# Attention scores of a head pair as two 64-row contractions in the two halves of the TensorE array

## The chip, the cores and the metric

The kernel runs on one core of one Trainium2 chip. The metric is device time in microseconds (us) of one execution, as the median of several runs. All times inside an execution come from one profiled execution, counted from the start of its span.

## What is computed

One layer of a hybrid model over 512 latent tokens (a grid of 8 rows by 64 columns) with 256 context tokens: a normalised input is projected, and two branches run in parallel, a state-space recurrence with a gated unit, and neighbourhood attention with 8 heads of 64 channels. The branches are merged and projected, and an expert retrieval (PEER) follows. The change lies in the attention. Cut from the reference to that:

```python
def na_mixer(q, k, v, k_ctx, v_ctx, rpb):
    ...
        s_lat = jnp.einsum('bhqd,bhkd->bhqk', q_row, k_band).astype(jnp.float32) * scale + bias
        s_ctx = jnp.einsum('bhqd,bhkd->bhqk', q_row, k_ctx).astype(jnp.float32) * scale
        prob = jax.nn.softmax(jnp.concatenate([s_lat, s_ctx], axis=-1), axis=-1).astype(v.dtype)
        return (jnp.einsum('bhqk,bhkd->bhqd', prob[..., :n_band], v_band)
                + jnp.einsum('bhqk,bhkd->bhqd', prob[..., n_band:], v_ctx))
```

The contraction over `d` has 64 terms for each head.

## The kernel before

**Where attention stands.** The whole layer is one program. A scheduler orders the instructions of every engine ahead of time from a timeline of its own; on the chip each engine then takes its instructions in that fixed order and waits where a semaphore is not set. The projections of keys, values and queries (`project`, L453) run on TensorE (PE) while VectorE (DVE) walks a recurrence of 95 dependent steps (`scan_step`, L588 to L595, four small operations on the tile `E` for each step). After its last step the states are copied from `E` to `S` (L618 on POOL, L619 on ScalarE, ACT), and the pool of `E` is closed. The space then holds `Y`, `gt` and `k0`, the tiles of `y_load` and `y_part` (L636 to L661), the readout of the recurrence: eight parts, each with one load of `gt` and eight small loads of `k0` on the SP queue, two buffers of each, and 12 matmuls into the bank `yy` (L657).

**The attention loop.** The 32 items are 4 tiles of 128 queries by 8 heads, heads fastest. For an item i, `att_a(i)` (L677) computes scores: 128 queries by 256 neighbourhood keys (L685) and by 256 context keys (L686) into one of the three `mm` banks; DVE adds the bias tile `bs` (L687) and takes the negated row maximum `nm` (L689); ACT takes the exponential into `P` (L691). `att_b(i)` transposes `P` in four pieces on PE into a `tp` bank (L698), and ACT and DVE copy a half each to `PT` (L700, L701). `att_c` multiplies `PT` by the values for the two heads of a pair at once: 8 matmuls, alternating between the lower and the upper 64 output rows (L716), into bank `kk` or `mc`. After eight heads `att_norm` divides by the sums (L719 to L734). The loop issues `att_b(i)`, `att_a(i + 2)`, now and then a `y_part`, then `att_c(i)`.

**The query tiles.** A 128-row tile of `kT` holds the keys of two heads, 64 rows each. Each head has a query tile of its own, `qT[h]`, 128 rows of which 64 are zero (memset on POOL, L628; copy on ACT, L629). So a score matmul contracts 128 rows, half of them against zeros:

```python
        ql = qT[h][:, m * 128:(m + 1) * 128]
        pe.matmul(s_[:, 0:256], ql, kT[h // 2][:, m:m + 2].rearrange("p j x -> p (j x)"), start=True, stop=True)
        pe.matmul(s_[:, 256:512], ql, kC[h // 2], start=True, stop=True)
```

These are 4-byte (f32) operands, and the trace records one such matmul as two weight loads and two matmuls.

**What follows.** When all eight `y_part` are done, `Y` is transposed (L771, into `tp`), which ends the use of the space of `Y`; `cb2` and the tiles `wm2` of `mod2` (L787 to L792: SP load, POOL product, ACT sum, two buffers, 32 times) come into the same space. Beside that the gated unit, the two branches and the merge run: 128-row matmuls of 512 columns in one helper (L445 to L447), whose weights are split by ACT and DVE (L174, L175). The order puts some of these matmuls into the end of the attention, ahead of the transposes of `Y`.

Of the kernel before, what the change touches and what calls it, by code (L numbers as in the profile page):

```python
# [10 lines left out]
F32 = mybir.dt.float32  # L11
# [5 lines left out]
AF = mybir.ActivationFunctionType  # L17
ALU = mybir.AluOpType
AX = mybir.AxisListType
# [15 lines left out]
NH = 8  # L35
# [51 lines left out]
def tile_hybrid(ctx, tc, A, out, dbg=None):  # L87
    nc = tc.nc
    sy, act, dve, gp, pe = nc.sync, nc.scalar, nc.vector, nc.gpsimd, nc.tensor

    def open_pool(**kw):
        cm = tc.tile_pool(reuse_waits="tile", **kw)
        return cm, cm.__enter__()

    def close_pool(*cms):
        for cm in cms:
            cm.__exit__(None, None, None)
# [13 lines left out]
    def bank(tag="mm", bufs=None):  # L111
        bufs = bufs or nb[tag]
        return (psA if tag in ("kk", "yy") else ps).tile([128, 512], F32, tag=tag, name=tag, bufs=bufs)
# [25 lines left out]
    ftcm, ftp = open_pool(name="ftp", bufs=1)  # L139
# [230 lines left out]

    def outer(eng, o, P, yr, yi, g0, n, tag, neg, pool):
        tmp = [pool.tile([128, n, TC, HG], F32, tag=f"{tag}{i}", name=f"{tag}{i}") for i in range(2)]
        xr, xi = (P[:, j, g0:g0 + n].rearrange("p g (m o) -> p g m o", o=1).to_broadcast([128, n, TC, HG])
                  for j in range(2))
        yr, yi = (y[:, g0:g0 + n].rearrange("p g (o h) -> p g o h", o=1).to_broadcast([128, n, TC, HG])
                  for y in (yr, yi))
        ov = [o[:, :, j].rearrange("p g (m h) -> p g m h", h=HG) for j in range(2)]
        cmul(eng, ov[0], ov[1], xr, xi, yr, yi, tmp, conj=neg)
# [197 lines left out]
    for o in SEQ1:  # L576
        m = nxt[o]
        nxt[o] += 1
        if o == "u":
            a, c = (a1, c1) if m == 1 else project(m, True)  # L580
# [21 lines left out]
    kT = [t[:, 0:640].rearrange("p (j x) -> p j x", x=128) for t in kTC]  # L602
    kC = [t[:, 640:] for t in kTC]
    Vt = [ftp.tile([128, 4, 512], F32, tag="ft", name=f"V{i}", bufs=4) for i in range(2)]
    V = [Vt[i // 4][:, i % 4] for i in range(7)]
    for m in range(4):
        a, c = project(8 + m, True)
# [3 lines left out]
        for j0, n in ((0, 4), (4, 3)):  # L611
            p = bank("tp")
# [5 lines left out]
        gp.tensor_copy(S[0:64, r], E[0:64, r, :, CC:CC + CL])  # L618
        act.copy(S[64:128, r], E[64:128, r, :, CC + CL - 1:CC - 1:-1])  # L619

    qt = [ftp.tile([128, 4, 512], F32, tag="ft", name=f"q{i}", bufs=4) for i in range(2)]
    qT = [qt[i // 4][:, i % 4] for i in range(NH)]
    for m in range(4):
        a, _ = project(12 + m, False)
        av = a.rearrange("p (r j c) -> p r j c", r=8, c=16)
        for e in range(2):
            s, z = slice(64 * e, 64 * e + 64), slice(64 * (1 - e), 64 * (1 - e) + 64)
            gp.memset(qT[2 * m + e][z], 0.0)  # L628
            act.activation(qT[2 * m + e][s].rearrange("p (j r c) -> p r j c", r=8, c=16), av[s], AF.Copy, scale=0.125)  # L629
    close_pool(ecm)  # L630

    ycm, yp = open_pool(name="yp", bufs=1, side="right")
# [32 lines left out]
    acm, ap_ = open_pool(name="ap", bufs=1)  # L665
    items = [(m, h) for m in range(4) for h in range(NH)]
    Pt, PTt, Ob, ssums = {}, {}, {}, {}

    def att_bias(i):
        m, h = items[i]  # L670
        bs = ap_.tile([128, 256], F32, tag="bs", name="bs", bufs=4)
        act.dma_start(bs, A["bias"][h, {0: 0, 3: 2}.get(m, 1)])
        return bs

    bss = {i: att_bias(i) for i in range(2)}

    def att_a(i):  # L677
        m, h = items[i]
        if h == 0:
            ssums[m] = ap_.tile([128, NH], F32, tag="ssum", name="ssum", bufs=2)  # L680
        if i + 2 < len(items):
            bss[i + 2] = att_bias(i + 2)
        s_ = bank()
        ql = qT[h][:, m * 128:(m + 1) * 128]
        pe.matmul(s_[:, 0:256], ql, kT[h // 2][:, m:m + 2].rearrange("p j x -> p (j x)"), start=True, stop=True)  # L685
        pe.matmul(s_[:, 256:512], ql, kC[h // 2], start=True, stop=True)  # L686
        dve.tensor_add(s_[:, 0:256], s_[:, 0:256], bss.pop(i))  # L687
        nm = ap_.tile([128, 1], F32, tag="nm", name="nm", bufs=4)
        dve.tensor_reduce(nm, s_, axis=AX.X, op=ALU.max, negate=True)  # L689
        P = ap_.tile([128, 512], F32, tag="P", name="P", bufs=2)  # L690
        act.activation(P, s_, AF.Exp, bias=nm, accum_out=ssums[m][:, h:h + 1])  # L691
        Pt[i] = P

    def att_b(i):
        P = Pt.pop(i)
        pt = bank("tp")
        for j in range(4):
            pe.transpose(pt[:, j * 128:(j + 1) * 128], P[:, j * 128:(j + 1) * 128], ident)  # L698
        PT = ap_.tile([128, 512], F32, tag="PT", name="PT", bufs=PTB)
# [36 lines left out]
    y_load(0)  # L736
    y_load(1)
    att_a(0)
    att_a(1)
    for i in range(len(items)):  # L740
        att_b(i)
        if i + 2 < len(items):
            att_a(i + 2)
        if i % 3 == 2 and i // 3 < 8:
            y_part(i // 3)
        att_c(i)
        if i % NH == 1 and i > NH:
            att_norm(i // NH - 1)
# [17 lines left out]
    for i in range(4):  # L766
        p = bank("tp")
# [76 lines left out]
    for o in MERGE:  # L844
        m = cnt[o]
# [106 lines left out]
    for half in range(2):  # L952
        p = bank("tp")
# [256 lines left out]
    av = gup[0].tile([128, 128], F32, name="av")  # L1210
# [88 lines left out]
    prev = None  # L1299
# [80 lines left out]
```

## Time and profile before

| | |
|---|---|
| median of 3 runs | 1874.2 us (1873.22 to 1884.75) |
| the profiled execution, its own time | 1876.31 us |
| its span, first to last instruction | 1874.5 us |
| PE, DVE, ACT, POOL busy over the span | 92%, 80%, 43%, 35% |
| attention, first transposes of `P` to last | 245.9 to 325.6 us |
| last step of the recurrence | 284.9 us |
| first and last part of the readout on PE | 312.4 and 350.6 us |
| last transposes of `Y` | 355.7 us |

A stretch of the program is read by the view that gives each engine's busy time in it, then by the chain of work that ended last, then by the timeline of the engine that the chain names. Matmuls overlap in the records (the duration of one is longer than the step to the next), so the cost of a group on PE is read from the chain, where pieces stand end to start.

### The profile page before, as it was taken

How to read it: one execution, taken by the hardware profiler on the slowest of the kernel's cores; microseconds unless marked ns; L12 is line 12 of the kernel's file. 1: busy time of each engine (PE TensorE's matmuls, PEld its weight loads, DVE VectorE, ACT ScalarE, POOL GpSimd, SP SyncE). 2: the span in 40 equal slices, each digit the busy share in tenths (PEclk: the TensorE clock that was granted, in tenths of full speed). 3: DMA queues.
4: the chain of work that ended last, by engine and by line, in shares of the span. 5: the costliest groups of instructions: out<-in, count | busy, mean ns of one | idle time of the engine just before them, and what ended most of it. 6: DMA issues, size and time to landing. Idle time of an engine off the chain costs nothing.

```text
span 1874.5 us, 27846 instructions
## 1 busy us (share of the span) xinstructions
PE 1727.8 (92%) x9941; PEld 1505.1 (80%) x9941; DVE 1499.0 (80%) x3111; ACT 808.0 (43%) x1276; POOL 659.0 (35%) x500
## 2 busy tenths in 40 slices
PE   4989879989999989997479999999999999999997
PEld 1778657767779989986369899999999999998885
DVE  7899995587669998999879788788888888884445
ACT  5362245455555435666433333333333333333333
POOL 3553201166523730010233445444445544440002
PEclk8999989999999999998589999999999999999998
DMA  7342114576744435757599899999999999994432
GB/s 278 114 135 83 62 54 112 175 262 210 254 147 148 143 110 159 216 172 212 146 383 361 293 331 329 341 353 350 321 344 357 319 338 347 327 346 144 127 113 79
DMA packets 186331, 426.18 MB, mean 227 GB/s; under 512 B 25552, under 2 KB 91216, under 8 KB 186192
## 3 DMA queue, kind: packets, MB, share of 16 engines
q1 hardware_dynamic: 84816, 231.44, 36.5%
q0 software_dynamic: 36864, 134.23, 20.0%
q10 hardware_dynamic: 64512, 58.73, 9.7%
q8 instruction: 78, 1.28, 0.3%
q14 instruction: 61, 0.50, 0.1%
HBM read 388.72 MB, written 35.62 MB: 226 GB/s over the span
## 4 chain that ended last, share of the span: by engine, by line
PE 71%; DVE 18%; DMA 4%; issue 3%; ACT 2%; POOL 2%; ACTq 0%; SPq 0%; DVEq 0%; POOLq 0%
PE acc L1251 9%; PE acc L1252 9%; PE acc L1253 9%; PE yy L447 5%; PE yy L445 5%; PE yy L446 5%; PE kk L447 5%; PE kk L445 5%; PE kk L446 5%; PE mm L447 2%; PE mm L446 2%; PE mm L445 2%; DVE E L595 2%; DVE ta L592 1%; DVE ta L594 1%
## 5 line engine op out<-in xcount | busy, mean ns | idle before, releaser
L174 ACT CAST whi<-wraw 128x1024 fp32r<-128x1024 f32 (+1 forms) x212 | 213.6, 1008 | 165.5 <-issue 49.9
L175 DVE TENSOR_TENSOR wlo<-wraw,whi 128x1024 fp32r<-128x1024 f32 (+1 forms) x174 | 225.1, 1294 | 56.9 <-ACT whi L174 49.4
L1134 POOL DMA_INDIRECT gu<-in_pu_dram,idx x128 | 173.8, 1357 | 262.5 <-DVE gj L1141 217.4
L1134 POOL DMA_INDIRECT gu<-in_pv_dram,idx x128 | 167.0, 1305 | 161.1 <-DVE gacc L1152 135.4
L1233 DVE TENSOR_TENSOR wlo<-wraw,whi 128x1024 fp32r<-128x1024 f32 x128 | 157.5, 1231 | 41.4 <-ACT whi L1232 37.6
L1152 DVE SCALAR_TENSOR_TENSOR gacc<-gu,av,gacc 128x1024 f32<-128x1024 f32 x127 | 162.6, 1281 | 25.5 <-DMA gu<-in_pv_dram,idx 25.0
L447 PE MATMUL yy<-hth,wlo 128*128 128x384 f32 x512 | 174.9, 342 | 3.6 <-DVE wlo L175 3.6
L1141 DVE SCALAR_TENSOR_TENSOR gj<-gu,hrow 128x1024 bf16<-128x1024 f32 x128 | 156.0, 1219 | 23.4 <-DMA gu<-in_pu_dram,idx 22.9
L445 PE MATMUL kk<-hth,whi 128*128 128x384 f32 x512 | 173.3, 338 | 1.0 <-ACT ring L932 1.0
L445 PE MATMUL yy<-hth,whi 128*128 128x384 f32 x512 | 173.9, 340 | 0.0
L446 PE MATMUL yy<-htl,whi 128*128 128x384 f32 x512 | 173.9, 340 | 0.0
L447 PE MATMUL kk<-hth,wlo 128*128 128x384 f32 x512 | 172.9, 338 | 0.6 <-DVE wlo L175 0.5
L446 PE MATMUL kk<-htl,whi 128*128 128x384 f32 x512 | 172.7, 337 | 0.0
L1232 ACT CAST whi<-wraw 128x1024 fp32r<-128x1024 f32 x128 | 134.0, 1047 | 81.5 <-PE yy L446 30.8
L175 POOL TENSOR_TENSOR wlo<-wraw,whi 128x1024 fp32r<-128x1024 f32 x38 | 96.1, 2532 | 91.5 <-ACT whi L174 87.8
L1120 ACT ACTIVATE gs<-mm 128x512 f32<-128x512 f32 x96 | 95.1, 1088 | 61.4 <-PE mm L1118 59.6
L791 POOL TENSOR_TENSOR wm<-wm,cb 128x1024 f32<-128x1024 f32 x32 | 82.4, 2575 | 87.8 <-DMA wm<-in_wmodT_dram 43.2
L447 PE MATMUL mm<-hxh,wlo 128*128 128x512 f32 x256 | 102.2, 399 | 6.6 <-DVE wlo L175 6.6
L445 PE MATMUL mm<-hxh,whi 128*128 128x512 f32 x256 | 100.0, 395 | 2.6 <-ACT whi L174 2.6
L447 PEld LDWEIGHTS yy<-hth,wlo 128*128 128x128 f32 x512 | 97.2, 190 | 5.7 <-DVE wlo L175 4.2
L446 PE MATMUL mm<-hxl,whi 128*128 128x512 f32 x256 | 100.8, 394 | 0.0
L445 PEld LDWEIGHTS kk<-hth,whi 128*128 128x128 f32 x512 | 96.4, 188 | 3.6 <-ACT ring L932 1.6
(2079 smaller groups left out, 4636.7 us busy)
## 6 DMA issues: line engine op xcount, KB each, us to landing
wraw<-in_puT_dram SPq DMA_DIRECT2D x128, 512.0 KB
wraw<-in_pv_dram SPq DMA_DIRECT2D x128, 512.0 KB
Gt_d<-gs ACTq DMA_DIRECT2D x24, 1024.0 KB
gch<-Gt_d ACTq DMA_DIRECT2D x32, 768.0 KB
wraw<-in_win_dram SPq DMA_DIRECT2D x32, 512.0 KB
wm<-in_wmodT_dram SPq DMA_DIRECT2D x32, 512.0 KB
wraw<-in_wq_dram SPq DMA_DIRECT2D x32, 512.0 KB
wm<-in_wm_dram SPq DMA_DIRECT2D x16, 512.0 KB
```

The costliest lines, as they stand in the source:

```text
L174: act.copy(hi[:, :kn], raw[:, :kn])
L175: i = eng.tensor_sub(lo[:, :kn], raw[:, :kn], hi[:, :kn].bitcast(F32))
L445: pe.matmul(o, hi[:, k], xh, start=(k == 0), stop=False)
L446: pe.matmul(o, hi[:, k], xl, start=False, stop=False)
L447: pe.matmul(o, lo[:, k], xh, start=False, stop=(k == kn - 1))
L1134: gp.indirect_dma_start(out=u, out_offset=None, in_=A[tab], in_offset=bass.IndirectOffsetOnAxis(ap=ix[:, s:s + 1], axis=0))
L1141: dve.scalar_tensor_tensor(jk, u, 1.0, hrow, op0=ALU.mult, op1=ALU.mult, accum_out=av[:, s:s + 1])
L1152: dve.scalar_tensor_tensor(gacc, u, av[:, s:s + 1], gacc, op0=ALU.mult, op1=ALU.add)
L1233: dve.tensor_sub(lo, w, hi.bitcast(F32))
L1251: pe.matmul(acc[t][half], wh_[:, ts], hi[:, cs], start=(j == 0), stop=False)
L1252: pe.matmul(acc[t][half], wh_[:, ts], lo[:, cs], start=False, stop=False)
L1253: return pe.matmul(acc[t][half], wl_[:, ts], hi[:, cs], start=False, stop=(j == 127))
```

## The change

The zero halves go: one query tile `qt` has the queries of both heads of a pair in its 128 rows. `att_a` now does a head pair: two `mm` banks, and four matmuls that contract 64 rows each, in the order (first head, neighbourhood), (second head, neighbourhood), (first, context), (second, context), tied in that order by `issue_after`. Then bias, maximum and exponential follow for the first and for the second head. `P` has three buffers instead of two. The loop calls `att_a` for every second item. The arithmetic of bias, softmax and values is unchanged.

```diff
-    qt = [ftp.tile([128, 4, 512], F32, tag="ft", name=f"q{i}", bufs=4) for i in range(2)]
-    qT = [qt[i // 4][:, i % 4] for i in range(NH)]
+    qt = ftp.tile([128, 4, 512], F32, tag="ft", name="qt", bufs=4)
     for m in range(4):
         a, _ = project(12 + m, False)
-        av = a.rearrange("p (r j c) -> p r j c", r=8, c=16)
-        for e in range(2):
-            s, z = slice(64 * e, 64 * e + 64), slice(64 * (1 - e), 64 * (1 - e) + 64)
-            gp.memset(qT[2 * m + e][z], 0.0)
-            act.activation(qT[2 * m + e][s].rearrange("p (j r c) -> p r j c", r=8, c=16), av[s], AF.Copy, scale=0.125)
+        act.activation(qt[:, m].rearrange("p (j r c) -> p r j c", r=8, c=16),
+                       a.rearrange("p (r j c) -> p r j c", r=8, c=16), AF.Copy, scale=0.125)
...
-        if i + 2 < len(items):
-            bss[i + 2] = att_bias(i + 2)
-        s_ = bank()
-        ql = qT[h][:, m * 128:(m + 1) * 128]
-        pe.matmul(s_[:, 0:256], ql, kT[h // 2][:, m:m + 2].rearrange("p j x -> p (j x)"), start=True, stop=True)
-        pe.matmul(s_[:, 256:512], ql, kC[h // 2], start=True, stop=True)
-        dve.tensor_add(s_[:, 0:256], s_[:, 0:256], bss.pop(i))
-        nm = ap_.tile([128, 1], F32, tag="nm", name="nm", bufs=4)
-        dve.tensor_reduce(nm, s_, axis=AX.X, op=ALU.max, negate=True)
-        P = ap_.tile([128, 512], F32, tag="P", name="P", bufs=2)
-        act.activation(P, s_, AF.Exp, bias=nm, accum_out=ssums[m][:, h:h + 1])
-        Pt[i] = P
+        for e in (2, 3):
+            if i + e < len(items):
+                bss[i + e] = att_bias(i + e)
+        ss_ = [bank() for _ in range(2)]
+        prev = None
+        for c in range(2):
+            for e in range(2):
+                r = slice(64 * e, 64 * e + 64)
+                k = (kC[h // 2][r] if c else
+                     kT[h // 2][r, m:m + 2].rearrange("p j x -> p (j x)"))
+                with tc.issue_after(prev) if prev is not None else ExitStack():
+                    prev = pe.matmul(ss_[e][:, c * 256:c * 256 + 256], qt[r, h // 2, m * 128:(m + 1) * 128], k,
+                                     start=True, stop=True).ins
+        for e in range(2):
+            s_ = ss_[e]
+            dve.tensor_add(s_[:, 0:256], s_[:, 0:256], bss.pop(i + e))
+            nm = ap_.tile([128, 1], F32, tag="nm", name="nm", bufs=4)
+            dve.tensor_reduce(nm, s_, axis=AX.X, op=ALU.max, negate=True)
+            P = ap_.tile([128, 512], F32, tag="P", name="P", bufs=3)
+            act.activation(P, s_, AF.Exp, bias=nm, accum_out=ssums[m][:, h + e:h + e + 1])
+            Pt[i + e] = P
...
     att_a(0)
-    att_a(1)
     for i in range(len(items)):
         att_b(i)
-        if i + 2 < len(items):
+        if i % 2 == 0 and i + 2 < len(items):
             att_a(i + 2)
```

The scheduler places everything around the attention anew. On PE, the two heads 6 and 7 of the first query tile stand so in the order before (L685 and L686 the two score matmuls of a head, L698 the transposes, L716 the values):

```order
L685 MATMUL mm_3028<-kTC3_2394,q1_2704 128x256
L686 MATMUL mm_3028<-kTC3_2394,q1_2704 128x256
L716 MATMUL kk_2922<-PT_2954,V0_2401 64x128
L698 MATMUL tp_3018<-ident_66,P_2965 128x128 x4
L685 MATMUL mm_3046<-kTC3_2394,q1_2704 128x256
L686 MATMUL mm_3046<-kTC3_2394,q1_2704 128x256
```

and so after the change (all score matmuls are now L688, the transposes L703; `mm_3017` is head 6, `mm_3018` head 7, `mm_3087` the first head of the next pair):

```order
L688 MATMUL mm_3017<-kTC3_2394,qt_2703 128x256
L703 MATMUL tp_3005<-ident_66,P_2957 128x128 x4
L688 MATMUL mm_3018<-kTC3_2394,qt_2703 128x256
L688 MATMUL mm_3017<-kTC3_2394,qt_2703 128x256
L688 MATMUL mm_3018<-kTC3_2394,qt_2703 128x256
L688 MATMUL mm_3087<-kTC0_2205,qt_2703 128x256
```

The first matmul of the pair stands apart from the other three, with transposes between. It is so in all 16 pairs: with three banks, the bank of the second head comes free later than that of the first. In one pair (heads 2 and 3 of the third query tile) the second stands apart as well.

On DVE, at the end of the recurrence, the first bias addition and maximum of the attention stood at the step whose product is `tb__2042` and do so no more (lines with a minus are the order before):

```order
 L593 TENSOR_TENSOR tb__2042<-E,L_78 128x64
-L687 TENSOR_TENSOR mm<-mm,bs 128x256
 L594 TENSOR_TENSOR ta<-ta,tb__2042 128x64
-L689 TENSOR_REDUCE nm<-mm 128x1
 L595 TENSOR_TENSOR E<-E,ta 128x64
```

The first pair is now five steps later, at `tb__2072`, and the work between the steps that follow is thinner:

```order
 L593 TENSOR_TENSOR tb__2072<-E,L_78 128x64
-L687 TENSOR_TENSOR mm<-mm,bs 128x256
+L692 TENSOR_TENSOR mm<-mm,bs 128x256 x2
 L594 TENSOR_TENSOR ta<-ta,tb__2072 128x64
-L701 COPY PT<-tp 128x256
-L689 TENSOR_REDUCE nm<-mm 128x1
-L595 TENSOR_TENSOR E<-E,ta 128x64
-L687 TENSOR_TENSOR mm<-mm,bs 128x256 x2
+L694 TENSOR_REDUCE nm<-mm 128x1 x2
+L595 TENSOR_TENSOR E<-E,ta 128x64
```

From here to the last step of the recurrence 13 steps are left in both orders (the one at `tb__2072` with them). Before, that last step stood behind the maxima of 19 items; now it stands behind those of 8, with 5 half copies of `PT` between.

On PE, the first part of the readout stood behind the scores of item 30 of 0 to 31 before (L657, four rows of one part):

```order
L698 MATMUL tp_3718<-ident_66,P_3670 128x128 x4
L685 MATMUL mm_3770<-kTC3_2394,q1_2704 128x256
L686 MATMUL mm_3770<-kTC3_2394,q1_2704 128x256
L657 MATMUL yy_2967<-k0__2863,X_736 64x128 x2
L657 MATMUL yy_2967<-gt_2861,S_737 64x128 x4
```

and now stands behind those of item 17 (L653):

```order
L703 MATMUL tp_3305<-ident_66,P_3234 128x128 x4
L688 MATMUL mm_3335<-kTC0_2205,qt_2703 128x256
L688 MATMUL mm_3334<-kTC0_2205,qt_2703 128x256
L688 MATMUL mm_3335<-kTC0_2205,qt_2703 128x256
L653 MATMUL yy_2964<-k0__2850,X_736 64x128 x2
L653 MATMUL yy_2964<-gt_2848,S_737 64x128 x4
```

All eight parts now lie within the attention, one to a head pair. Of the 512-column matmuls of what follows, 90 stood ahead of the last transposes of `Y` before and 60 do now. From the scores of the expert retrieval on, the order of PE is as before.

## Rows read from the trace of the kernel before

**Rows 1.** Page, part 1: busy time, share of the span, instructions.
```profile
PE 1727.8 (92%) x9941; PEld 1505.1 (80%) x9941; DVE 1499.0 (80%) x3111; ACT 808.0 (43%) x1276; POOL 659.0 (35%) x500
```

**Rows 2.** Busy time by stretch: length, PE, PEld, DVE, ACT, POOL, PEclk, DMA, GB/s.
```profile
230.00:240.00 10.00, 0.00 (x0) 0.00 (x0) 9.00 (x39) 0.00 (x0) 0.00 (x0) 0.51 0.00 0
240.00:250.00 10.00, 4.08 (x12) 3.27 (x12) 9.35 (x38) 4.02 (x7) 0.00 (x0) 0.50 0.06 17
...
260.00:270.00 10.00, 10.00 (x72) 7.06 (x70) 9.10 (x31) 4.41 (x12) 0.61 (x1) 1.00 0.22 67
...
300.00:310.00 10.00, 10.00 (x74) 7.59 (x75) 6.76 (x15) 4.74 (x15) 0.61 (x1) 1.00 0.42 124
```

**Rows 3.** Chain that ended last, 251 to 356 us: start, length, piece.
```profile
252.36 0.43 PE mm L686 x2
252.79 0.59 PE kk L716 x8
253.38 0.59 PE tp L698 x4
253.96 0.43 PE mm L685 x2
...
258.68 1.02 PE kk L716 x14
...
267.83 0.63 PE mm L685 x2
...
270.06 0.36 PE mc L716 x2
...
274.35 0.44 PE tp L698 x4
...
337.57 1.46 PE yy L657 x24
...
344.06 1.46 PE yy L657 x24
...
355.68 0.65 PE tp L771 x8
356.35 3.91 DMA cb<-in_cv_dram
```

**Rows 4.** Timeline of DVE, 241 to 285 us.
```profile
241.11 0.27 DVE L592 TENSOR_TENSOR ta<-E,L 128x64 f32<-128x64 f32 x1
...
242.15 0.27 DVE L592 TENSOR_TENSOR ta<-E,L 128x64 f32<-128x64 f32 x1
...
248.92 0.42 DVE L687 TENSOR_TENSOR mm<-mm,bs 128x256 f32<-128x256 f32 x1
...
250.49 0.75 DVE L687 TENSOR_TENSOR mm<-mm,bs 128x256 f32<-128x256 f32 x2
...
251.50 1.28 DVE L689 TENSOR_REDUCE nm<-mm 128x1 f32<-128x512 f32 x2
...
252.83 0.42 DVE L701 COPY PT<-tp 128x256 f32<-128x256 f32 x1
...
284.92 0.27 DVE L595 TENSOR_TENSOR E<-E,ta 128x64 f32<-128x64 f32 x1
```

**Rows 5.** Timeline of ACT, 243 to 291 us.
```profile
243.79 1.28 ACT L691 ACT_TABLE_LOAD   x1 [22.93 <-DVE nm L689]
...
287.11 1.91 ACT L619 COPY S<-E 64x2048 f32<-64x2048 f32 x1
```

**Rows 6.** Loads of the readout on SP, by source line.
```profile
L643 SPq DMA_DIRECT2D k__2863<-Kd x8: 303/424/498, 291.3 to 304.8; - x8
L643 SPq DMA_DIRECT2D k__2874<-Kd x8: 302/424/1547, 306.6 to 313.1; - x8
```

**Rows 7.** What follows the attention: busy time, columns as in rows 2.
```profile
356.00:512.00 156.00, 143.34 (x611) 112.91 (x608) 117.59 (x88) 87.69 (x143) 92.50 (x38) 0.99 0.70 238
```

**Rows 8.** Loads of `mod2` on SP, by source line: ns, first and last start.
```profile
L789 SPq DMA_DIRECT2D wm<-in_wmodT_dram x32: 327/328/425, 356.7 to 497.7; - x32
```

## Prediction

> **What bounds the kernel now.** I read the page first: PE is busy 92% of the span, DVE 80% [rows 1]. Such shares mix stages, so next I read the busy time of the stretches around the attention [rows 2]. The reader is to see three regimes. From 230 to 240 us PE does nothing, DVE walks the recurrence, and PE's granted clock is 0.51, its lower level (1.2 GHz). From 240 to 250 the attention begins, still at 0.50. From 260 on PE is busy for 10.00 of 10 us at the full clock, while DVE falls from 9.10 to 6.76. The chain of waits says the same: from about 252 to 356 us it runs through PE, piece to piece [rows 3]. So the attention is bound by PE, and the change takes work off the engine that binds.
>
> What the attention hands on is the end of the transposes of `Y`, at 355.68 + 0.65 = 356.3 us [rows 3]. Right behind it the chain leaves PE for the load of `cb`, and the 32 loads of `mod2` follow from 356.7 to 497.7 us, one every 4.55 us on two buffers [rows 8]. PE in that stage has 611 records, some 597 of them matmuls of 512 columns [rows 7]. One costs 0.24 us: 21 of them stand between the end of one readout part, 337.57 + 1.46 = 339.03, and the next at 344.06 [rows 3]. That is 143 of 156 us, so PE has some 13 us of slack there and the loads set the pace. I therefore count how far the end of the transposes of `Y` moves.
>
> **What PE's pieces cost** [rows 3]. Four transposes take 0.44 us behind scores and 0.59 behind values; scores 0.43 for each of the two matmuls, 0.63 for the first one behind values; one value matmul 0.36, seven 1.02. So a change between whole-array work and work in the column halves costs 0.15 to 0.20, a transpose 0.11, seven values 0.87, one 0.21, a readout part 1.31. The order has 90 such changes from the first transposes to the last of `Y`. The sum of before: transposes 14.1 and 1.8 (16 of the sums), scores of 30 heads 26.0, values 16 × 1.08 = 17.3, readout 10.5, transposes of `Y` 2.0, changes 90 × 0.15 = 13.5, and 90 matmuls of 512 columns 21.6: 106.8. Some 2.7 of it ran before 251.3 us, which leaves 104.1, where the trace has 356.3 - 251.3 = 105.0. The list can be trusted.
>
> These changes are also where the Trainium skill speaks against this edit: its page "TensorEngine Tiling (Array Packing)", section Key Properties, says that a change of tiling mode drains the engine. The trace agrees, with the 0.15 to 0.20 us above; had the 90 changes cost nothing, the list would give 91 and not 105.
>
> **Term 1, the scores: -8.** Before, a head's two matmuls take 0.87. What two 64-row halves do side by side no row shows. The nearest is the values, which alternate between the column halves: 14 records in 0.87 us are 0.062 each, where a transpose, with as many columns, takes 0.11. So alternate halves overlap almost twofold there. Without overlap the scores stay at 26.0; with all of it they fall to 13.0. I take a staircase, because PE begins records in order and each score matmul is two records of 0.22: an alternating matmul behind another adds 0.22, and a lone one costs 0.43. The order leaves the first of each pair alone, so a pair is 0.43 + (0.43 + 2 × 0.22) = 1.30; in six places the next pair's first follows directly and adds only 0.22. 15 pairs: 19.5 - 1.3 = 18.2.
>
> The same page, section Theoretical Speedup, gives up to a factor of two for a contraction of 64. By it the scores would come to the 13.0 and the sum below to 5 us less; the order, with its lone first matmuls, speaks against that.
>
> **Term 2, the changes: +0.6.** There are 90 again, 26 of them into the new row halves. I take 0.15 for each; 0.20 for the 26 would be 1.3 more, and I add half.
>
> **Term 3, matmuls moved behind the transposes of `Y`: -7.2 there.** 60 instead of 90 stand ahead: 30 × 0.24. They come back in the next stage, in its 13 us of slack; I charge 1 us there, between 0 and 7.2.
>
> **Term 4, the recurrence goes first: +11.6.** Before, the first bias addition stood five steps earlier. An addition and a maximum take half of 0.75 + 1.28, so 1.0 us, which stood ahead of the addition at 248.92 and no longer do [rows 4]; the first addition is now at about 247.9 and the first maximum ends at 249.3. Behind it come the table load of 1.28 us [rows 5] and the exponential, so the first transposes start at 251.5. PE's list of after is 14.1 + 1.8 + 18.2 + 17.3 + 10.5 + 2.0 + 13.5 + 14.4 = 91.8. But DVE now gives it only eight items until the recurrence ends: four pairs at 0.75 + 1.28, five copies of 0.42 and 12.5 steps of 1.04 [rows 4] are 8.1 + 2.1 + 13.0 = 23.2, so the last step is at 271 us (284.92 before). Then ACT copies the states, twice 1.91 [rows 5], with the next copy of `PT` queued behind it, and the values of the third pair wait for that until 276. Until then PE can do 28 transposes (3.1), four pairs of scores (4.8), values of two pairs and a first (2.4) and 17 changes (2.6): 12.9 of 24.5 us, so 11.6 idle. Before, PE was busy throughout that stretch: 17 maxima stood between those steps.
>
> **Term 5, new waits: +4.** Scores of a pair now end together, and the first transposes need two additions, two maxima and an exponential behind them: 0.75 + 0.6 + 0.7 is 2.1 us. Between stand values, transposes and a lone score, 1.0 + 0.6 + 0.6, which just covers it. Where two pairs follow each other, with only three banks, it doesn't. Bounds 0 and 8 (0.6 a pair); I take 4, a third of a microsecond for each of 12 pairs. The gone memsets and the shorter copies of queries lie beside DVE's recurrence, at 230 to 250 us, and are worth nothing.
>
> **Sum.** The transposes of `Y` end at 251.5 + 91.8 + 0.6 + 11.6 + 4 = 359.5 us, 3.2 later than 356.3. With 1 us of term 3 the end moves by +4, from 1876.3 us of the profiled execution to 1880. That execution lies 2.1 above the median of the runs, so I forecast a median of 1878 us. So the expected 8 us are earned on PE and spent again where DVE comes first.
>
> **Rivals.**
> *PE's work decides, 1866 us.* If DVE keeps up (the lead items' transposes and scores slip into the recurrence, waits of terms 4 and 5 are 4 and not 15.6), `Y` is done at 348 and the end is 12 us earlier than forecast. For it: PE was busy 10.00 of 10 us against a DVE at 9.10 [rows 2]. Against: 12.5 steps and eight items are all that DVE's order has there.
> *The halves don't overlap, 1886 us.* Scores stay at 26.0: +8. For it: weights of 128 columns are loaded for each record, where those of the values have 64. Against: 0.062 us for alternating values.
> *The readout's loads hold up the attention, 1890 us.* All eight parts now stand inside the attention, in PE's fixed order, one every pair (some 5.9 us with the part). The first two loads took from 291.3 to 313.1 us [rows 6], 21.8, since each small load waits for another queue's; from 276 that ends at 298, and the first two parts are due at about 296 and 300. Eight parts that come 1.5 us late each are +12. It decides once the loads of a part need more than the 5.9 us. Against: seven gaps from 312.4 to 350.6 us were 5.5 each, beside other loads.
> *The clock, 1885 us.* PE starts at the lower level, as at 240 to 250, and with gaps it may stay there until 276: 12.9 us of work become 25.8, more than the 24.5 that there are, with 4 us lost to chains and 2 to the later rise: +7.
>
> **Chances.** Forecast 0.45, PE's work 0.22, no overlap 0.13, loads 0.12, clock 0.08. The forecast's own range is 1871 to 1885. The range for 8 in 10, 1863 to 1890, takes in the first rival with 3 us below it, and the upper ones up to the loads; their sums with one another stay out. About 1% (19 us) can be told from no change. Faster by that would need all of terms 4 and 5 gone and the scores at 13.0: 0.03. Slower needs two upper rivals together: 0.07. Within 1%: 0.90.
>
> **What would show it.** Right: last step of the recurrence near 271, its states copied by 276; PE idle for some 10 us between 251 and 276; three score matmuls in about 0.87 us behind a lone 0.43; last transposes of `Y` near 359. Wrong: a last step later than 277, scores of a pair at 1.7, PE waiting for loads of `k0` or `gt`, a clock of 0.5 beyond 260, or a stage after `Y` that doesn't follow its start.

## The result, and the profile after

The changed kernel takes 1884.8 us (median of 8 runs, 1880.7 to 1891.8), the kernel before beside it 1874.1 (8 runs): ratio 1.0056, with a 95% interval of 1.0038 to 1.0073. That is 10.5 us slower (7 to 14), within 1% as forecast, and at the upper end of the forecast's own 1871 to 1885. The forecast was 1878, so +4 us. The time lies in the range; what it is made of was forecast otherwise, as the rows show. The profiled execution took 1884.7 us, 1883.0 of them the span. The page's first part has next to the same busy times as [rows 1]:

```profile
PE 1724.4 (92%) x9941; PEld 1500.0 (80%) x9941; DVE 1497.6 (80%) x3111; ACT 805.0 (43%) x1272; POOL 659.2 (35%) x492
```

The busy time by stretch, with the columns of [rows 2]: length, PE, PEld, DVE, ACT, POOL, PEclk, DMA, GB/s.

```profile
240.00:250.00 10.00, 0.00 (x0) 0.00 (x0) 9.31 (x37) 1.48 (x2) 0.00 (x0) 0.50 0.14 49
250.00:260.00 10.00, 9.36 (x32) 5.74 (x34) 7.94 (x32) 3.81 (x11) 0.00 (x0) 0.50 0.10 30
260.00:270.00 10.00, 7.94 (x60) 5.49 (x56) 9.15 (x34) 4.08 (x12) 1.06 (x1) 0.84 0.18 55
270.00:280.00 10.00, 10.00 (x59) 6.76 (x58) 5.22 (x12) 7.06 (x12) 3.26 (x3) 0.73 0.40 112
280.00:290.00 10.00, 8.42 (x69) 5.84 (x68) 7.20 (x18) 5.75 (x19) 0.00 (x0) 1.00 0.49 138
...
356.00:512.00 156.00, 142.17 (x608) 112.84 (x606) 112.96 (x88) 88.54 (x144) 91.44 (x38) 0.99 0.68 230
```

Read the PEclk column first. From 250 to 260 us PE is busy for 9.36 of 10, but with 32 records at 0.50 (1.2 GHz); the kernel before does 10.00 with 72 records from 260 on, at 1.00 [rows 2]. In the two rows from 260 to 280 the level is mixed: by stretches of 1 us it is full from 262 to 269, low again to 275.5, and full from there on. PE's timeline shows the two levels and the wait between them (start, length, piece, in brackets the idle time before it and what ended it):

```profile
259.54 1.97 PE L721 MATMUL kk<-PT,V 128*64 128x128 f32 x14
...
264.82 1.09 PE L721 MATMUL kk<-PT,V 128*64 128x128 f32 x14
...
268.92 1.11 PE L703 MATMUL tp<-ident,P 128*128 128x128 f32 x4 [2.06 <-ACT P L696]
```

The chain of waits of the same stretch gives the durations at either level (start, length, piece):

```profile
250.64 1.11 PE tp L703 x4
251.75 2.00 PE mm L688 x6
...
268.08 0.79 ACT P L696 x2
268.92 1.11 PE tp L703 x4
270.03 2.00 PE mm L688 x6
272.03 1.90 PE kk L721 x14
...
276.22 0.59 PE tp L703 x4
276.81 1.06 PE mm L688 x6
277.87 1.02 PE kk L721 x14
278.88 0.59 PE tp L703 x4
279.47 0.63 PE mm L688 x2
...
353.90 1.15 PE tp L775 x16
355.06 5.08 DMA cb<-in_cv_dram
```

Four transposes take 1.11 us at 250.64 and 268.92, 0.59 at 276.22; three alternating score matmuls (six records) 2.00 and 1.06. So the level fell a second time: PE worked at the higher one before a wait of 2.06 us for `P` that ended at 268.92 (fourteen records of the values in 1.09 us at 264.82), and from there to 275.5 at the lower. The transposes of `Y` end at 353.90 + 1.15 = 355.06 us, 1.3 earlier than in [rows 3]. So at this point the changed kernel is ahead, but it has done less: 60 of the 512-column matmuls stand ahead of it and not 90, and the other 30 (7.2 us) are still to come. What follows loses the lead. By source line, with the first and last start of its instructions: the output projection's first product (L894; L890 before) and the transposes of `x1` (L922; L918 before), of the changed kernel:

```profile
L894 PE MATMUL mm<-woh,mgh x64: 387/389/505, 502.6 to 553.2; 128*128 128x512 f32 x64
L922 PE MATMUL tp<-ident,x x32: 270/272/328, 540.3 to 579.8; 128*128 128x128 f32 x32
```

and of the kernel before:

```profile
L890 PE MATMUL mm<-woh,mgh x64: 387/389/632, 496.7 to 548.2; 128*128 128x512 f32 x64
L918 PE MATMUL tp<-ident,x x32: 270/272/328, 533.9 to 573.6; 128*128 128x128 f32 x32
```

1.3 us ahead at 355 are 5.9 behind at the output projection and 6.4 at the transposes of `x1`; the span ends 8.5 later (1883.0 against 1874.5). The last load of `mod2` starts 1.7 us later than in [rows 8]:

```profile
L793 SPq DMA_DIRECT2D wm<-in_wmodT_dram x32: 327/328/730, 356.9 to 499.4; - x32
```

Two questions follow: what the lower level costs and why it lasts, and what gave the lead back behind `Y`.

### The profile page after: what moved, and what is told of

Same layout as the page of the kernel before. It is cut to its first block, busy times and chain, and to the rows that moved or that the text cites. A ratio compares the mean times of both kernels' runs of the same rounds, so it can differ in the third digit from the quotient of the medians.

```text
span 1883.0 us, 27825 instructions
## 1 busy us (share of the span) xinstructions
PE 1724.4 (92%) x9941; PEld 1500.0 (80%) x9941; DVE 1497.6 (80%) x3111; ACT 805.0 (43%) x1272; POOL 659.2 (35%) x492
## 4 chain that ended last, share of the span: by engine, by line
PE 68%; DVE 17%; DMA 6%; issue 3%; ACT 3%; POOL 2%; SPq 0%; ACTq 0%; DVEq 0%; POOLq 0%
PE acc L1255 9%; PE acc L1256 9%; PE acc L1257 9%; PE yy L447 5%; PE yy L445 5%; PE yy L446 5%; PE kk L447 5%; PE kk L445 5%; PE kk L446 5%; PE mm L447 2%; PE mm L445 2%; DVE E L595 2%; PE mm L446 2%; DVE ta L592 2%; DMA wor<-in_wout_dram 2%
## 5 line engine op out<-in xcount | busy, mean ns | idle before, releaser
L175 DVE TENSOR_TENSOR wlo<-wraw,whi 128x1024 fp32r<-128x1024 f32 (+1 forms) x174 | 238.5, 1371 | 56.2 <-ACT whi L174 55.9
L1138 POOL DMA_INDIRECT gu<-in_pv_dram,idx x128 | 174.2, 1361 | 153.7 <-DVE gacc L1156 123.9
L175 POOL TENSOR_TENSOR wlo<-wraw,whi 128x1024 fp32r<-128x1024 f32 x38 | 96.8, 2550 | 97.7 <-ACT whi L174 94.0
```

The costliest lines, as they stand in the source:

```text
L175: i = eng.tensor_sub(lo[:, :kn], raw[:, :kn], hi[:, :kn].bitcast(F32))
L1138: gp.indirect_dma_start(out=u, out_offset=None, in_=A[tab], in_offset=bass.IndirectOffsetOnAxis(ap=ix[:, s:s + 1], axis=0))
```

## Experiments

The times are compared with the kernel before in the same rounds (medians 1874 to 1876 us). For each kernel the stretch from the first transposes of `P` to the last of `Y` is split by rows of 10 us, counted from its start: idle is length less busy time, the price of the lower level is the busy time times (1 - PEclk), since half of the work's speed is missing at 0.50, and the rest is work at the full level. The last column but one counts the 512-column matmuls that stand ahead of the last transposes of `Y` in PE's order; at 0.24 us each they are a part of the work, so the work of two kernels compares directly only where they are as many.

| kernel | first P transposes | last Y transposes | idle | lower level | work | matmuls ahead | ratio to before |
|---|---|---|---|---|---|---|---|
| before | 245.9 | 356.3 | 1.3 | 2.2 | 106.8 | 90 | 1 |
| changed | 250.6 | 355.1 | 5.4 | 8.7 | 90.4 | 60 | 1.0056 |
| changed, again (e12) | 249.3 | 354.0 | 7.8 | 6.0 | 90.8 | 60 | 1.0044 |
| e1 single rows | 243.6 | 371.0 | 2.7 | 15.5 | 109.2 | 90 | 1.0090 |
| e2 pairs whole | 250.3 | 351.9 | 2.5 | 2.3 | 96.8 | 53 | 1.0022 |
| e3 first pair by head | 245.5 | 351.5 | 7.4 | 8.1 | 90.4 | 54 | 0.9976 |
| e5 single, warm | 245.4 | 359.6 | 2.0 | 1.6 | 110.6 | 90 | 1.0006 |
| e6 first pair, warm | 244.8 | 349.2 | 6.0 | 6.7 | 91.6 | 54 | 0.9946 |
| e7 changed, warm | 251.7 | 356.6 | 6.3 | 5.3 | 93.3 | 60 | 1.0040 |
| e8 early, warm | 235.8 | 360.3 | 12.9 | 7.7 | 103.9 | 90 | 1.0041 |

**The two parts of the change, apart.** Run e1 takes row halves without pairs:

```diff
...
-        ql = qT[h][:, m * 128:(m + 1) * 128]
-        pe.matmul(s_[:, 0:256], ql, kT[h // 2][:, m:m + 2]...)
+        r = slice(64 * (h % 2), 64 * (h % 2) + 64)
+        ql = qt[r, h // 2, m * 128:(m + 1) * 128]
+        pe.matmul(s_[:, 0:256], ql, kT[h // 2][r, m:m + 2]...)
...
```

> One part of the change alone: 64-row contractions and the single query tile without zeros, but head by head in the loop of before, so that the two matmuls of a head stand in the same half of the array one behind the other. PE's and DVE's orders are those of the kernel before, instruction by instruction. Theory 'start' (row halves are worth 8 us on PE only where they alternate, and the changed kernel lost that and 10 us more because the recurrence goes first, with PE waiting and at its lower clock from 251 to 276 us): two score matmuls still take 0.87 us, nothing moves, time within 4 us of before. Rival 'halves' (work in row halves costs something itself, in changes of mode of 0.15 to 0.20 us into and out of them or in the weight loads): 64 more changes between halves and whole array would show as +3 to +10 us over before.

Measured: ratio 1.0090 (1.0077 to 1.0103), 17 us over before with the same order on PE and DVE. Theory "start" falls: it had no loss here. Rival "halves" had one, but of 3 to 10 us, and 17 is outside that. The busy time of PE alone (length, PE, PEclk, DMA, GB/s) shows why:

```profile
250.00:260.00 10.00, 10.00 (x35) 0.50 0.16 45
260.00:270.00 10.00, 10.00 (x38) 0.50 0.09 30
270.00:280.00 10.00, 10.00 (x50) 0.69 0.14 39
280.00:290.00 10.00, 10.00 (x69) 1.00 0.18 54
```

PE is busy without a gap from 250 us on and stays at its lower level until some 276, with 35 and 38 records in 10 us for the 72 of [rows 2]. What brings the level up at 276 no run here shows. The kernel before, in the same order with whole-array scores, is at the full level from 251 on:

```profile
250.00:260.00 10.00, 9.64 (x69) 0.97 0.34 103
```

Of 17 us, 15.5 - 2.2 = 13.3 are the lower level.

Run e2 takes the pairs and turns without row halves:

```diff
-                r = slice(64 * e, 64 * e + 64)
+                r = slice(0, 128)
-                    prev = pe.matmul(..., qt[r, h // 2, m * 128:(m + 1) * 128], k, ...)
+                    prev = pe.matmul(..., qT[h + e][:, m * 128:(m + 1) * 128], k, ...)
```

> The other part alone: the changed kernel's pairs, the two heads' matmuls in the same turn, but with query tiles that have zero halves, so that every score matmul takes all 128 rows. The recurrence goes first on DVE as in the changed kernel. Theory 'start': the overlap is lost, 15 pairs x (1.74 - 1.30) = 6.6 us more PE work than the changed kernel, so 8 to 20 us above before (after was 10.8 above it); PE again at the lower clock to about 270 us. Rival 'halves' (the row halves are what costs): the time falls back to that of before or to within 5 us of it.

Measured: 1.0022 (1.0012 to 1.0031), 4 us over before and so 6 below the changed kernel, although PE has 6.4 us more work (96.8 against 90.4) with seven 512-column matmuls fewer in it, so that whole-array scores cost some 8 us more where 6.6 were expected. The level is full from 255 us on and costs 2.3 and not 8.7. PE alone:

```profile
250.00:260.00 10.00, 9.66 (x54) 0.75 0.14 40
260.00:270.00 10.00, 9.56 (x76) 1.00 0.26 68
```

So the expectation of theory "start" fails here too, and rival "halves" has the number. But this run is no clean test: the scheduler has written DVE's order anew as well. The first addition stands where the changed kernel has it, but 14 maxima and 12 copies of `PT` come before the last step of the recurrence, not 8 and 5, and the idle time is 2.5 us, not 5.4. The clean pair is e1 and the run that follows.

**Row halves with a start in whole rows.** In run e5 the 8 heads of the first query tile keep tiles with zero halves, in the kernel of e1; orders are the same word for word.

```diff
-        r = slice(64 * (h % 2), 64 * (h % 2) + 64)
+        r = slice(64 * (h % 2), 64 * (h % 2) + 64) if m >= 1 else slice(0, 128)
-        ql = qt[r, h // 2, m * 128:(m + 1) * 128]
+        ql = qt[r, h // 2, m * 128:(m + 1) * 128] if m >= 1 else qz[:, m, h]
```

> The kernel of run e1_single_rows (row halves, head by head, orders of the kernel before; 15.1 us above before, its clock at 0.50 until 276 us with PE busy 10.00 of 10 us from 250 on), with one edit: the 8 heads of the first query tile take query tiles with zero halves, so 16 of the 64 score matmuls use all 128 rows, the other 48 keep their 64. PE's and DVE's orders are unchanged. Theory 'clock' (PE at work in halves of the array is left at its lower level, whole-array scores bring it up): full clock from about 252 us as in before, 12 to 15 us less than that run, so -3 to +4 us against before. Rival 'halves' (each record in a row half costs by itself): a quarter of the loss goes with a quarter of the records, 4 us less, +9 to +13 us against before.

Measured: 1.0006 (0.9998 to 1.0015): the loss is gone with a quarter of the records. PE alone:

```profile
240.00:250.00 10.00, 4.48 (x14) 0.55 0.11 28
250.00:260.00 10.00, 9.26 (x67) 1.00 0.35 100
260.00:270.00 10.00, 10.00 (x67) 1.00 0.21 58
```

Full level from 249 on, and it stays there when the row halves come. The mean granted clock of the whole execution says the same of every run: 0.951 to 0.958 in the 5 of e1, 0.962 to 0.967 in the 11 of e5. This pair of runs shows theory "clock". Rival "halves" has a small part of its own: where they don't alternate, row halves make the work 2.4 us longer than before in e1 and 3.8 in e5 (why it is more in e5, with fewer of them, stays open). The Trainium skill, "TensorE: Matmul & The Clock Gate", Part 1, says that the lower level is the default and that activity releases it. By that rule e1, busy for 10.00 of 10 us, would have risen as before did; it didn't, and the measurement decides.

**The first pair head by head.** Run e3 changes only the turns of the first pair, and the first addition stands again at step 78 of the recurrence:

```diff
-        for c in range(2):
-            for e in range(2):
+        for x in range(4):
+                c, e = (x % 2, x // 2) if i < 2 else (x // 2, x % 2)
```

> The changed kernel with one edit: the first pair's four score matmuls go head by head instead of in turn, all other pairs alternate as in the changed kernel. By the order the first bias addition then stands again five steps of the recurrence earlier, as in the kernel before, and eight more of the attention's heads come on DVE between the steps. Theory 'start': first transposes near 246 us, full clock from about 252, waits up to 276 gone: 8 to 18 us below the changed kernel, so -8 to +3 us against before. Rival 'halves': the time stays at that of the changed kernel, +8 to +12 us against before. Rival 'next stage' (the changed kernel lost its time behind the transposes of Y, by another order of the matmuls there): between the two, and the stretch from the last transposes of Y to the first matmul of the output projection is the same 147 us.

Measured: 0.9976 (0.9965 to 0.9987). The number is as "start" has it, but the level is full only from 257 us, the lower one costs 8.1 us, and it falls again from 284 to 291, behind a wait of 2.51 us for a copy of `PT` that is queued behind the copies of the states. PE's timeline at the rise:

```profile
254.07 1.12 PE L703 MATMUL tp<-ident,P 128*128 128x128 f32 x4
255.12 1.95 PE L688 MATMUL mm<-kTC,qt 64*128 64x256 f32 x6
256.99 0.65 PE L721 MATMUL kk<-PT,V 128*64 128x128 f32 x6
257.58 0.65 PE L703 MATMUL tp<-ident,P 128*128 128x128 f32 x4
```

The transposes of `Y` end 4.8 us ahead of before, with 36 matmuls fewer ahead of them; the output projection starts 0.6 ahead (496.1), and 7 of the 9.4 us by which this span is shorter appear between 597 and 970 us, where the scheduler has written another order on PE, DVE and ACT. So this time isn't the attention's alone.

Run e6 adds the whole-array first query tile to e3, in the same order:

> The kernel of run e3_first_pair_by_head (5.4 us below before; clock full from about 256.5 us, low again from 284 to 291 after a wait of 2.5 us for a copy of PT behind the copies of the states), with the 8 heads of the first query tile on all 128 rows; orders unchanged. Theory 'clock': full from about 251 us, 3 us earlier behind a start at 245.5, against 4 pairs x 0.44 = 1.7 us more PE work: 0 to 3 us below that run, -9 to -5 us against before. Rival 'halves': 1.7 us from the lost overlap and nothing gained: 1 to 3 us above that run, -4 to -2 us against before.

Measured: 0.9946 (0.9928 to 0.9964), 10 us below before and the fastest of all. The level is full from 250 us, as "clock" has it, then falls from 280 to 287, behind the same wait. The medians of e3 and e6 are 3.6 us apart, their profiled spans 0.3 (1865.1 and 1865.4), and the output projection starts at 496.1 in e3 and 496.2 in e6, so this gain isn't certain; against both given kernels e6 is faster.

Run e7 gives the changed kernel the whole-array first tile, with its late first addition kept:

> The changed kernel with the 8 heads of the first query tile on all 128 rows, in the same pairs and turns, the first addition on DVE still behind step 83 of the recurrence. DVE's order behind it shifts a little towards the attention (7 more heads before the last step). Theory 'clock': full from about 254 us as in run e2_pairs_whole and no second fall, 6 to 11 us below the changed kernel, 0 to +5 us against before. Rival 'waits' (the recurrence first and the values behind the state copies cost the changed kernel its gain, as terms 4 and 5 of the prediction say): at most 2 us below the changed kernel, +8 us or more against before. Rival 'halves': 1 to 3 us above the changed kernel.

Measured: 1.0040 (1.0022 to 1.0058), 3 us below the changed kernel, an interval that overlaps with its own. Neither theory has this: the lower level costs 3.4 us less, but idle time and work grow by 0.9 and 2.9, and the first transposes come 1.1 later. The order behind the first pair shifted, so it is no clean test of the changed kernel's share; e1 and e5 are.

**Behind the transposes of `Y`.** Run e4 leaves out 32 matmuls of the changed kernel, e11 the same 32 of the kernel before: the second product of four row blocks in eight gate projections.

```diff
-        pe.matmul(o, hi[:, k], xl, start=False, stop=False)
+        if not (fewer[0] and k < 4):
+            pe.matmul(o, hi[:, k], xl, start=False, stop=False)
```

> The changed kernel without 32 of the matmuls of 512 columns in the stage behind the transposes of Y: the second of the three products (high part of the weight, low part of the input) is left out for 4 of 8 row blocks in the projections of the last four blocks of both gates. Orders are otherwise those of the changed kernel. It asks what term 3 of the prediction assumed. Theory 'PE sets the pace there': 32 x 0.24 = 7.7 us less at the first matmul of the output projection and at the end, so 6 to 8 us below the changed kernel, +3 to +5 us against before. Rival 'loads set the pace' (13 us of slack, as predicted): 0 to 1.5 us below the changed kernel.

> The kernel before without the same 32 matmuls of 512 columns that e4_32_matmuls_fewer leaves out of the changed kernel (second of the three products, 4 of 8 row blocks, last four blocks of both gates). Theory 'two chains' (behind the transposes of Y the 32 loads of mod2 and PE's gates run side by side, and in the traces so far the first transposes of x1 come at the later of 28 us behind the last product of mod2 and 34.5 us behind the first matmul of the output projection; in before the loads are the later by 2.6 us): the first matmul of the output projection 4 to 8 us earlier than 496.7, the last product of mod2 still near 506, first transposes of x1 still near 534, time -2 to 0 us against before. Rival 'PE sets the pace there': everything 6 to 8 us earlier, -8 to -6 us against before.

> The changed kernel once more, word for word, beside runs of before of the same call, to see which of the distances in its first profile come again. Theory 'two chains': last transposes of Y near 355, full clock not before 262 us and low again behind the state copies, first matmul of the output projection near 502, first transposes of x1 between 537 and 540, +9 to +11 us against before. Rival: the 3 us between the two chains' 537 and the 540.3 of the first profile don't come again, and the time is +5 to +8 us.

Measured: e4 1.0035 (1.0023 to 1.0048), e11 0.9991 (0.9981 to 1.0002), e12 1.0044 (1.0028 to 1.0060). The same two lines, of e4:

```profile
L899 PE MATMUL mm<-woh,mgh x64: 387/389/497, 499.5 to 549.5; 128*128 128x512 f32 x64
L927 PE MATMUL tp<-ident,x x32: 270/272/330, 536.8 to 576.8; 128*128 128x128 f32 x32
```

of e11:

```profile
L895 PE MATMUL mm<-woh,mgh x64: 387/389/501, 492.8 to 546.6; 128*128 128x512 f32 x64
L923 PE MATMUL tp<-ident,x x32: 271/272/329, 529.9 to 570.0; 128*128 128x128 f32 x32
```

and of e12:

```profile
L894 PE MATMUL mm<-woh,mgh x64: 387/389/505, 501.8 to 551.3; 128*128 128x512 f32 x64
L922 PE MATMUL tp<-ident,x x32: 270/272/328, 538.1 to 578.4; 128*128 128x128 f32 x32
```

32 x 0.24 = 7.7 us of PE work taken away move the output projection by 3.9 us in before (496.7 to 492.8) and by 2.3 to 3.1 in the changed kernel (501.8 and 502.6 to 499.5). A part of that stood there before: the last transposes of `Y` are 1.0 us earlier in e11 than in before, and 1.1 earlier in e4 than in the changed kernel's first profile. Counted from them it is 2.9, and 2.0 to 2.3. So neither "PE sets the pace" (7.7) nor "loads set the pace" (0 to 1.5) holds: between a quarter and four tenths comes through. Theory "two chains" of e11 has the time (-1.7 us), but its mechanism falls: the transposes of `x1` came 4.0 us earlier, where it had them stay near 534. In e12 most distances come again: transposes of `Y` done at 354.0, output projection at 501.8, 9 us in the median. Its level is low from 249.3 to 262 us. The second fall isn't there, where the wait was 1.49 us and not 2.06, nor is it in e4, whose attention is the same; so it belongs to one profile of three. And the transposes of `x1` start at 538.1, 2 us before the 540.3 of the first profile. In e4 and e11 the order of the stages farther down is another than in the kernels that they are made from, so the output projection's row counts here, and the end less.

**Candidates.** PE does nothing from 225 to 245 us. Run e8 starts the attention earlier on DVE:

```diff
+    att_a(0)
+    with tc.issue_after(lastA[0]):
+        scan_step(70)
+    for i in range(2):
+        step(i)
+    for p_ in range(70+1, NCK):
+        scan_step(p_)
```

> A candidate: the kernel of e7_changed_warm with the recurrence's steps from 70 on written behind the attention's first two heads, and step 70 bound behind the first pair's maxima, so that the attention starts 9 us earlier on DVE (near 238 us) and more of its heads stand between the last steps. PE does nothing from 225 to 245 us in all kernels so far. Theory 'PE decides': the start is worth up to 8 us, -16 to -6 us against before. Rival 'late states': the recurrence ends later, near 295 us, the readout's eight loads of 5.2 us each follow it, and PE runs out of other work: -4 to +8 us against before. Rival 'clock': PE waits for DVE at the start, stays at its lower level and gains nothing: -5 to +2 us.

Measured: 1.0041 (1.0026 to 1.0055), as rival "late states" has it. PE alone:

```profile
240.00:250.00 10.00, 10.00 (x76) 0.98 0.23 72
...
320.00:330.00 10.00, 10.00 (x79) 1.00 0.85 184
330.00:340.00 10.00, 3.80 (x40) 0.79 0.68 198
340.00:350.00 10.00, 8.04 (x69) 0.69 0.66 167
350.00:360.00 10.00, 5.93 (x61) 0.65 0.31 84
```

The attention runs from 236 us, at the full level from 240, and is done by 314, but the recurrence ends at 294, and the readout's loads come behind it. PE's longest waits from 330 on:

```profile
PE yy L653 <- DMA k__3180<-Kd: 6.0, 1, 6.0
PE yy L653 <- DMA k__3461<-Kd: 3.3, 1, 3.3
```

Two runs then issue the loads of `k0` of the first two parts early, into room beside `qz`: e9 on e8's order with the start at step 74, e10 on e6.

```diff
+    for b in range(2):
+        for j in range(TC):
+            o = (TC - 1 - j) * HG
+            sy.dma_start(k0e[b][j * HG:(j + 1) * HG], Kd[b * 4:b * 4 + 4, :, o:o + 128]...)
```

> A second candidate, after run e8_early_warm (attention done at 313 us, but PE idle or at its lower level from 330 to 370, the recurrence's last step at 294 and the last readout part at 356; 7.5 us above before). Two edits to that kernel: step 74 of the recurrence is bound behind the first pair's maxima and not step 70 (first transposes near 240 us, last step near 287), and the 16 small loads of k0 of the first two readout parts are issued early into spare room beside the queries, so that behind the states only gt is loaded for them. Theory 'late states' (the chain of the readout's loads behind the recurrence is what starved PE there): the last readout part comes 15 to 20 us earlier, near 337, transposes of Y done near 345, -16 to -9 us against before. Rival 'loads of the other six parts set it anyway': last part near 350, -6 to +4 us.

> The kernel of run e6_first_pair_warm (10 us below before) with the 16 small loads of k0 of the first two readout parts issued early, as in e9_early_k0_ahead; the first addition stays where it is. Theory 'late states': PE waited only some 2 us for the readout there, so 0 to 3 us less than that run, -13 to -9 us against before. Rival 'loads set the end of Y': last readout part 10 us or more earlier and the end with it, -18 to -14 us.

Measured: e9 0.9993 (0.9983 to 1.0003), its last readout part at 346.6 us: place and time fit the rival, that the loads of the other six parts set it. e10 0.9962 (0.9950 to 0.9974): its last part is 8.5 us earlier than in e6, the last transposes of `Y` start at 343.0 and the output projection at 489.4, 7.3 ahead of before; but the end is not ahead of e6, since the stage from 600 to 960 us takes 7 us longer there, again in another order. Both theories of e10 miss the end.

## Why the prediction was right in its range and wrong in its terms

*The sum.* 10.5 us were measured where 4 were forecast, and 1884.8 lies 0.2 us inside the range. That it does is in part luck: the last transposes of `Y` came 1.3 us earlier than before and not 3.2 later, and what follows lost 9.8 us of the span (from -1.3 to +8.5) where 1 was charged.

*Bound by PE, work as listed: right.* The list had 106.8 us for before, and the rows give 106.8. For the changed kernel it had 91.8 + 0.6 = 92.4, and the rows give 90.4 (90.8 in e12).

*Term 1, the staircase: right.* Behind a lone first of 0.63 with its change of mode (0.43 and 0.20) three alternating matmuls take 1.06, a change of 0.15 to 0.20 and 0.86 to 0.91, where 0.87 was forecast. e2 points the same way: some 8 us more work without halves, for 6.6. Term 2 is inside the 2 us by which the list is off, and not tested by itself.

*Term 4, the recurrence first: the place right, the price wrong.* The first transposes came at 250.6 (251.5 forecast), the recurrence ended at 268.6 (271), and the last state copy on ACT started at 271.6. But PE was not idle for 11.6 us and 4 more in term 5: it was idle for 5.4 us in the whole stretch (7.8 in e12). It was slow instead. The forecast took PE's durations at the full level and compared 12.9 us of work with 24.5 us of time; at the lower level the same work fills them. The lower level cost 8.7 us (6.0 in e12), and 5.4 + 8.7 = 14.1 (13.8) stands where the terms had 15.6. So the right size is luck: idle time that was put 10 us too high, and a lower level of 9 us that was left out.

*The rival "the clock": its mechanism happened, with a chance of only 0.08.* Its number, 1885, is the one measured, but it was thought of as gaps that keep the level low. A gap stands ahead of the second fall (2.06 us up to 268.92); gaps don't explain the first stretch, since e1 has none from 250 on and is low for 26 us. What the argument lacked is that the work itself had changed: with scores in row halves PE's busy time no longer brought the level up as it did before. e1 and e5 show it, in one order: 17 us lost, and not lost with 16 whole-row matmuls at the start.

*Term 3, the 30 matmuls: mis-sized.* "13 us of slack" and "loads set the pace" were read from the busy sum of a stretch, and 1 of 7.2 us was charged. The stretch from the last transposes of `Y` to the output projection, split as in the table, has 12.6 us idle, 1.3 of lower level and 126.4 of work before, and 13.8, 1.6 and 132.2 in the changed kernel (12.6, 3.2 and 132.0 in e12). So the idle time didn't take the added matmuls in: PE waits as long as before, and 5.8 us of the 7.2 stand there as work. That is most of the 7.2 us by which the changed kernel falls back between the transposes of `Y` (-1.3) and the output projection (+5.9). The kernels of the table agree: with 90 matmuls ahead they have 125 to 126 us of work there, with 53 to 60 ahead 132 to 134, and idle time of 11 to 14 in both. e4 and e11 took out other matmuls, those of the last gate blocks; there idle time grew, to 16.0 and 17.8 us, and so less came through. One place of the changed kernel's idle time is seen in its chain:

```profile
371.44 3.40 DVE wlo L175
374.89 0.79 PE mm L447
```

The load of `cb` takes 5.08 us (5.04 in e12) for the 3.91 of [rows 3], ACT and DVE follow with `cth`, `cb` and the split of a weight, and PE waits 2.7 us for its low part `wlo`: from 370 to 380 it is busy for 5.84 us (7.09 in e12) against 9.88 before. Why the load is longer, and the last 2 to 3 us up to the end of the span, stay open.

*What the change earned and lost.* From the first transposes of before (245.9) to the output projection both splits can be added. The changed kernel has 10.6 us less work, starts 4.7 later, idles 5.3 more and loses 6.8 more to the lower level: +6.2, where its output projection starts 5.9 later (in e12 -10.4, +3.4, +6.5 and +5.7, so +5.2 for 5.1). So the gain on PE is there, and three losses of like size, the late start, the waits and the clock, take more than that back; the forecast had the first two, with the waits too high.

*The other rivals.* "The halves don't overlap" is out by term 1. "The readout's loads hold up the attention" didn't happen: PE waited 0.5 us for them in the changed kernel; it became true in e8, where the states come late. "PE's work decides" would have needed the idle time and the level of before.

## What to carry to other kernels

After a change that makes matmuls use half of the array, TensorE can stay at its lower clock level behind a pause, with no gap in the trace to show for it (26 us in e1): read the granted clock of each stretch beside the busy time, and price work there at the level that it will have. Here a start in whole rows (8 of 32 heads) bought the level back where the heads go one by one (e1 to e5, 16 us); where pairs alternate (e3 to e6, changed to e7), it gave a few us at most, and not for certain. Work that an order puts off isn't gained: count it where it comes back, and don't take idle time there for room (5.8 of 7.2 us came back). And where a scheduler writes the order, compare runs that share it (e1 with e5, e3 with e6), since a new order far downstream moved as much time as the change did.

## Not expected

TensorE, busy for 10.00 of 10 us, stayed at 0.50 from 250 to 270 us and on to 276 with matmuls of 64 rows, of 64 columns and transposes in the mix (e1), and rose within 5 us of its start in the same order with 128-row scores (before, e5). Once up, it stayed up through 48 score matmuls of 64 rows (e5). After waits of 2.06 us (the changed kernel) and 2.51 (e3) it was low again for 6 to 7 us, after one of 1.5 (e7) for 3; after one of 1.49 (e12) it wasn't.
